# Moving one V unit into the attention loop, overlapping the closing part of a cross-covariance attention kernel, and halving its last store

## The chip, the cores and the metric

One core of one Trainium2 chip. The metric is the device time of one execution in microseconds. Each kernel is run several times; the profile ("the trace") comes from one execution and covers a span about 1.8 us shorter than the device time. For the kernel before, that execution is none of the timed runs quoted below: it took 144.34 us. Times quoted are medians of all runs. A run over 1.5% above the fastest of its kernel counts as slow and stays out of the ratios. A ratio is the mean time of one kernel's fast runs over the mean of the other's fast runs in the same rounds, so it is not quite the ratio of the medians quoted.

## The reference

```python
Q, K, V: (8, 12, 512, 64) float32
Q_norm = Q / (norm(Q, axis=-2) + 1e-10)          # norm over the 512 rows, per column
K_norm = K / (norm(K, axis=-2) + 1e-10)
attn   = einsum('bhnd,bhne->bhde', Q_norm, K_norm)          # 64 x 64 per head
attn   = softmax(attn, axis=-1)
out    = einsum('bhnd,bhde->bhne', V, attn)
```

The attention matrix is only 64 x 64 per head, but it needs all of Q and K of that head before any output of that head can be made. 96 heads are taken four at a time: 24 units.

## The kernel before

The engines: PE does the matmuls and PE transposes, ScalarE (ACT in the profile's lines), VectorE (DVE) and GpSimd (POOL) the elementwise work, SyncE (SP) issues the transfers. Matmul results land in PSUM, a small memory of which the kernel has few tiles; an eviction is the copy of outputs from PSUM to SBUF, from where they are stored.

Per unit there are two chains. The attention side: load Q and K (512 KB each), cast to bf16, gram matrices on PE, norms, scale, softmax. The V side: load V, cast (`cast_v`), eight PE transposes into PSUM and a copy out (`vtrans`), sixteen output matmuls and two evictions (`outs`), store. The program order is written by hand; the V side runs behind the attention at a rate that `outs_by` fixes.

```python
    vbp = ctx.enter_context(tc.tile_pool(name="vbp", bufs=3))
    ps_v = ctx.enter_context(tc.tile_pool(name="ps_v", bufs=1, space=bass.MemoryType.PSUM))   # one transposing tile
    ps_o = ctx.enter_context(tc.tile_pool(name="ps_o", bufs=2, space=bass.MemoryType.PSUM))
    def outs_by(s):
        return max(0, (s - 2) * 19 // 22)
    ...
    for s in range(U):                       # U = 24
        n0, n1 = outs_by(s - 1), outs_by(s)
        on(load_qk, s + LOAD_AHEAD)          # 3 ahead
        while nv < min(U, n1 + 3):
            load_v(nv); nv += 1
        while nst < n1 - 3:
            store(nst); nst += 1
        ...                                  # casts, grams, norms; outs(n0..n1-1); softmax; vtrans
    ...                                      # remaining loads and stores
    # closing part
    both = (nc.scalar.copy, nc.vector.tensor_copy)
    ...                                      # softmax of the last unit
    normalise(last - 1)
    doubled(last - 1)
    outs(n1)
    store(n1)
    normalise(last)
    doubled(last)
    for u in range(n1 + 1, U):
        cast_v(u, nc.vector.tensor_copy)
        vtrans(u)
        outs(u, both)
        store(u)
```

All loads and stores are issued by SyncE, in program order.

## Time and profile before

143.5 us (median of 4 runs, 142.95 to 145.23; the longest is a slow one, the mean of the other three is 143.3). What matters of its profile, with "E" for the start of the exponentials of unit 23, the last attention unit (all in us from the span's start):

| | before |
|---|---|
| span of the profiled run | 142.6 |
| Q of unit 23 landed / cast | 102.55 / 103.03 |
| E | 113.67 |
| last eviction ends | 138.88 (E + 25.2) |
| last store issued / landed | 138.95 / 141.72 |

The landing of a transfer is the last of its sixteen landing records in the trace, one for each DMA engine. A line of the timeline gives start, duration, engine, line of the kernel, operation, tiles as out<-in, and in brackets the idle time of the engine before it and what ended it. PEclk is the granted clock, the share of PE's full clock that the trace records, in tenths; it is 1.0 or 0.5. The page's busy shares say little here, as no engine is above 71%:

```profile
PE 89.9 (63%) x2232; PEld 70.0 (49%) x2232; DVE 101.3 (71%) x370; ACT 91.2 (64%) x159; POOL 42.3 (30%) x41
```

They average over a loop in which the transfers never pause and a closing part in which every engine mostly waits; the prediction below takes the two apart.

### The profile page before, as it was taken

Reading aid. Unit: us, or ns where it says so; the run is one execution under the profiler, and the core shown is the slowest. Engines: PE = TensorE matmul, PEld = TensorE weight load, DVE = VectorE, ACT = ScalarE, POOL = GpSimd, SP = SyncE. Lnnn points to the kernel's source line nnn. Section 1 sums busy time; section 2 is a strip of 40 time slices with the busy share of each in tenths; the row PEclk is TensorE's granted clock in tenths of the full one; section 3 lists DMA queues with packets and bytes.
Section 4 is the critical chain, followed back from the end, with each engine's and each line's share of the span. In section 5 each row is a group of like instructions: output and inputs, shape, how many; then the busy total and the mean of one; then the engine's idle time right before and its main releaser. Section 6 shows DMA issues by size and latency. Waiting matters only on the chain.

```text
span 142.6 us, 5388 instructions
## 1 busy us (share of the span) xinstructions
PE 89.9 (63%) x2232; PEld 70.0 (49%) x2232; DVE 101.3 (71%) x370; ACT 91.2 (64%) x159; POOL 42.3 (30%) x41
## 2 busy tenths in 40 slices
PE   0057746698675754889398955899559473544440
PEld 0046533586554543768285834687438342333320
DVE  0867399879999979989698999979997553123310
ACT  3013422498999965798879874998989853423340
POOL 8614233334422234442245223464321200000000
PEclk9999999999999999857975799658995955555555
DMA  4999999999999999999999999999999998533033
GB/s 176 315 406 406 398 409 410 398 399 402 401 405 403 417 401 415 395 407 413 407 416 405 407 414 408 411 407 408 405 403 404 398 402 336 221 150 142 29 123 147
DMA packets 19992, 50.67 MB, mean 355 GB/s; under 512 B 1536, under 2 KB 1536, under 8 KB 19968
## 3 DMA queue, kind: packets, MB, share of 16 engines
q1 hardware_dynamic: 19968, 50.34, 90.7%
q8 instruction: 17, 0.28, 0.8%
q14 instruction: 7, 0.06, 0.1%
HBM read 37.75 MB, written 12.58 MB: 353 GB/s over the span
## 4 chain that ended last, share of the span: by engine, by line
DVE 32%; PE 22%; POOL 17%; DMA 11%; issue 8%; ACT 4%; SPq 2%; POOLq 1%; ACTq 0%; DVEq 0%
POOL rq L111 17%; DVE scr L106 9%; DMA qf<-in_Q_dram 9%; PE po L163 7%; PE vps L145 6%; PE gram L94 6%; DVE kqs L116 5%; DVE ab L138 5%; DVE esum L134 5%; ACT vt L147 3%; DMA out_dram<-so 2%; DVE rinv L136 2%; PE lgdup L122 2%; DVE vb L87 2%; PE lgdup L152 2%
## 5 line engine op out<-in xcount | busy, mean ns | idle before, releaser
L111 POOL TENSOR_TENSOR rq<-nsq,mhalf 128x4 f32<-128x4 f32 x24 | 37.1, 1548 | 69.3 <-DVE nsq L106 69.3
L94 PE MATMUL gram<-qkb 32*128 32x128 bf16 x1536 | 36.7, 262 | 14.9 <-DVE qkb L83 9.7
L94 PEld LDWEIGHTS <-qkb 32*128 32x128 bf16 x1536 | 30.9, 117 | 16.5 <-DVE qkb L83 10.6
L147 ACT COPY vt<-vps 128x1024 bf16<-128x1024 bf16 x24 | 24.1, 1003 | 9.9 <-PE vps L145 9.6
L167 ACT COPY so<-po 128x512 f32<-128x512 f32 x43 | 23.3, 589 | 4.3 <-PE po L163 3.9
L106 DVE CUSTOM_DVE_ANT_0 scr<-gram,ident 128x128 f32<-128x128 f32 x96 | 21.9, 281 | 3.8 <-PE gram L94 3.6
L163 PEld LDWEIGHTS <-vt 128*64 128x64 bf16 x384 | 15.2, 136 | 19.1 <-ACT vt L147 11.8
L145 PE MATMUL vps<-identb,vb 128*128 128x128 bf16 x192 | 19.4, 260 | 6.6 <-DVE vb L87 5.6
L163 PE MATMUL po<-ab,vt 128*64 128x128 bf16 x384 | 19.8, 263 | 5.8 <-ACT vt L147 5.8
L80 DVE CAST qkb<-qf 128x1024 bf16<-128x1024 f32 x24 | 18.0, 749 | 7.1 <-DMA qf<-in_Q_dram 7.1
L87 ACT CAST vb<-vf 128x1024 bf16<-128x1024 f32 x19 | 19.9, 1046 | 2.9 <-DMA vf<-in_V_dram 2.9
L145 PEld LDWEIGHTS <-vb 128*128 128x128 bf16 x192 | 14.3, 116 | 10.1 <-DVE vb L87 6.8
L152 PE MATMUL lgdup<-ab,identb 64*64 64x256 bf16 x24 | 7.8, 324 | 17.3 <-DVE ab L138 17.1
L153 ACT CAST ab<-lgdup 64x256 bf16<-64x256 f32 x24 | 8.8, 368 | 14.1 <-PE lgdup L152 13.5
L83 DVE CAST qkb<-kf 128x1024 bf16<-128x1024 f32 x24 | 16.4, 683 | 0.0
L99 ACT COPY kq<-gram 64x256 f32<-64x256 f32 x24 | 8.8, 368 | 11.2 <-DVE nsq L106 10.9
L167 DVE COPY so<-po 128x512 f32<-128x512 f32 x5 | 3.5, 691 | 16.8 <-PE po L163 16.8
L122 PE MATMUL lgdup<-ident,kqs 64*64 64x64 f32 x96 | 11.4, 248 | 3.5 <-ACT ab L153 2.3
L126 DVE TENSOR_TENSOR sl<-lgdup,rq 64x256 f32<-64x256 f32 x24 | 9.9, 413 | 4.9 <-PE lgdup L122 4.7
L130 ACT ACTIVATE ex<-sl 64x256 f32<-64x256 f32 x24 | 10.0, 417 | 4.1 <-DVE sl L126 3.8
L116 DVE TENSOR_TENSOR kqs<-kq,rq 64x256 f32<-64x256 f32 x24 | 10.1, 422 | 2.3 <-POOL rq L111 0.8
L122 PEld LDWEIGHTS lgdup<-ident,kqs 64*64 64x64 f32 x96 | 7.0, 121 | 7.7 <-ACT ab L153 4.8
(16 smaller groups left out, 44.3 us busy)
## 6 DMA issues: line engine op xcount, KB each, us to landing
qf<-in_Q_dram SPq DMA_DIRECT2D x24, 512.0 KB, 10.1
kf<-in_K_dram SPq DMA_DIRECT2D x24, 512.0 KB, 10.1
vf<-in_V_dram SPq DMA_DIRECT2D x24, 512.0 KB, 10.1
out_dram<-so SPq DMA_DIRECT2D x24, 512.0 KB, 10.1
```

Source lines behind the costliest of these rows:

```text
L80: nc.vector.tensor_copy(qkb[u][:, :, 0:D], qf[u])
L83: nc.vector.tensor_copy(qkb[u][:, :, D:], kf[u])
L87: copy(w.rearrange("p s t d -> p s (t d)"), vf[u])
L94: nc.tensor.matmul(gbuf[:, h, 0:2 * D], x, x, start=(t == 0), stop=(t == R - 1), tile_position=(NV * h, 0))
L106: nc.vector.tensor_tensor_reduce(out=scr, in0=gbuf[:, h, 0:2 * D], in1=ident, scale=1.0, scalar=1e-20, op0=ALU.mult, op1=ALU.add, accum_ou ...
L111: nc.gpsimd.tensor_tensor(out=r, in0=n2, in1=mhalf, op=ALU.pow)
L116: nc.vector.tensor_tensor(out=kk[D:], in0=kq[u][D:], in1=rq[u][D:, :, None].to_broadcast([D, HU, D]), op=ALU.mult,)
L122: nc.tensor.transpose(lg[:, h, :], kqs[u][D:, h, :], ident[D:, D:])
L145: nc.tensor.transpose(ps[:, g, t, :], vb[u][:, g, t, :], identb)
L147: nc.scalar.copy(w, ps)
L163: nc.tensor.matmul(po[rows, t, :], vt[u][:, g, t, rows], a[:, 2 * g + x].rearrange("p a d -> p (a d)"), tile_position=(0, MV * x),)
L167: copies[g](s[:, g], po)
```

## The change

Its intent: do one more V unit in the loop (10/11 instead of 19/22 of the attention's rate: 19 units of outputs instead of 18), so that one unit less is left; in the closing part, put the cast and the transposes of a unit ahead of the outputs of the one before it, so that they overlap; halve the last store, so that less data follows the last eviction.

```diff
-    vbp = ctx.enter_context(tc.tile_pool(name="vbp", bufs=3))
+    vbp = ctx.enter_context(tc.tile_pool(name="vbp", bufs=4))
-        return max(0, (s - 2) * 19 // 22)
+        return max(0, (s - 2) * 10 // 11)
-    def store(u):
-        nc.sync.dma_start(out=Of[u], in_=so[u].rearrange("p s t d -> p s (t d)"))
+    def store(u, g=slice(0, SV)):
+        nc.sync.dma_start(out=Of[u][:, g], in_=so[u][:, g].rearrange("p s t d -> p s (t d)"))
     exps(last)
+    cast_v(n1 + 1, nc.vector.tensor_copy)
     normalise(last - 1)
     doubled(last - 1)
-    outs(n1)
+    vtrans(n1 + 1)
+    outs(n1, both)
     store(n1)
     normalise(last)
     doubled(last)
+    cast_v(n1 + 2, nc.vector.tensor_copy)
     for u in range(n1 + 1, U):
-        cast_v(u, nc.vector.tensor_copy)
-        vtrans(u)
+        if u + 1 < U:
+            vtrans(u + 1)
+        if u + 2 < U:
+            cast_v(u + 2, nc.vector.tensor_copy)
         outs(u, both)
-        store(u)
+        if u < last:
+            store(u)
+    for g in range(SV):
+        store(last, slice(g, g + 1))
```

## The prediction

> **What bounds the kernel now.** I read the page's forty slices first, to see where the span changes character, then the DMA issues of SyncE in order of time, then what ScalarE waits for at the end of the main loop, then one period of the closing part.
>
> ```profile
> PEclk9999999999999999857975799658995955555555
> DMA  4999999999999999999999999999999998533033
> GB/s 176 315 406 406 398 409 410 398 399 402 401 405 403 417 401 415 395 407 413 407 416 405 407 414 408 411 407 408 405 403 404 398 402 336 221 150 142 29 123 147
> ```
>
> A slice is 142.6/40 = 3.57 us. From slice 3 to slice 33, that is from 7 to 118 us, the DMA moves some 405 GB/s without a break; in the last seven slices it falls to a third. So there are two regimes: a main loop in which the transfers are always behind, and a closing part of about 25 us in which they are not. Next: who is slow in each.
>
> ```profile
> 92.51 0.34 SPq L68 DMA_DIRECT2D qf<-in_Q_dram  x1
> 93.77 0.49 SPq L69 DMA_DIRECT2D kf<-in_K_dram  x1
> 95.08 0.38 SPq L73 DMA_DIRECT2D vf<-in_V_dram  x1
> 96.37 0.39 SPq L76 DMA_DIRECT2D out_dram<-so  x1
> 97.55 0.37 SPq L73 DMA_DIRECT2D vf<-in_V_dram  x1
> ...
> 105.20 5.36 SPq L73 DMA_DIRECT2D vf<-in_V_dram  x3
> 110.61 28.71 SPq L76 DMA_DIRECT2D out_dram<-so  x9
> ```
>
> These are SyncE's issues. They come every 1.28 us, which is what 512 KB takes at 405 GB/s, and the page gives 10.1 us from issue to landing: eight transfers are always in flight and the ninth waits. So in the main loop a transfer lands according to its place in SyncE's order. The landing records of the trace say how close the compute is to them: Q of unit 10 is cast 6.3 us after it landed, Q of unit 20 0.07 us after, Q of unit 23 0.5 us after (landed 102.55, cast 103.03). An attention step takes 3.98 us (4.70 in a half-clock stretch), the four transfers of a step 5.1 us, so the loads' lead is used up just at the end.
>
> ```profile
> 105.22 1.05 ACT L87 CAST vb<-vf 128x1024 bf16<-128x1024 f32 x1 [0.52 <-DMA vf<-in_V_dram]
> 106.28 0.37 ACT L153 CAST ab<-lgdup 64x256 bf16<-64x256 f32 x1
> ```
>
> There the load is ahead on the path: the cast of V of unit 17 starts when it has landed (105.14), the copy behind it on ScalarE frees the PSUM tile for which the next logits wait (106.71), and grams, norms and exponentials of unit 23 follow without slack. The chain of waits runs through exactly these.
>
> ```profile
> 129.51 0.68 DVE L87 CAST vb<-vf 128x1024 bf16<-128x1024 f32 x1
> 130.25 1.03 PE L145 MATMUL vps<-identb,vb 128*128 128x128 bf16 x8 [1.39 <-DVE vb L87]
> 131.37 1.01 ACT L147 COPY vt<-vps 128x1024 bf16<-128x1024 bf16 x1 [2.31 <-PE vps L145]
> 132.44 1.06 PE L163 MATMUL po<-ab,vt 128*64 128x128 bf16 x16 [1.16 <-ACT vt L147]
> 133.12 0.59 ACT L167 COPY so<-po 128x512 f32<-128x512 f32 x1 [0.73 <-PE po L163]
> 133.55 0.69 DVE L167 COPY so<-po 128x512 f32<-128x512 f32 x1 [3.36 <-PE po L163]
> ```
>
> One unit of the closing part, in order of time. Nothing overlaps: cast, eight transposes, copy, outputs, eviction, and the next unit's cast comes only at 134.16, behind the eviction on VectorE. The period is 134.16 - 129.51 = 4.65 us, and there are five such units (19 to 23). Their inputs landed long before (V of unit 23 at 117.9, cast at 134.2), so this is pure latency.
>
> **What the Trainium skill says.** "TensorE: Matmul & The Clock Gate", Part 1: the PE clock is halved until about one window of 3.4 us has been busy. The trace agrees in kind: 0.5 from 114.9 us to the end, where PE works 2.1 us of 4.65. The same page, Part 4, says that transposes do not count as busy in the same way; half of the closing part's PE work is transposes, so I don't count on a warm clock there. "DMA: Bandwidth & Descriptors", Where 436 GB/s comes from: 435 GB/s is the fabric's ceiling; here 405 is the plateau, so the loop has no transfer rate to gain. The same page, Anatomy of one DMA (written for the GpSimd path): a fixed cost of about 2 us, mostly the receipt of the last write. The last store here is issued at 138.95 and has landed at 141.73, 2.8 us, of which 1.3 is the data.
>
> **The change part by part.**
>
> *Rate 10/11.* By the formula, 19 units of output instead of 18 are done in the loop, so 20 V units instead of 19 are cast and transposed there. One unit moves from the closing part. But from step 17 on one more V load and one more store stand in SyncE's order ahead of Q and K of units 21 to 23: 2 x 1.28 = 2.57 us. Setting the new order against the landing times of the same places gives Q 21, 22, 23 at 95.02, 100.07, 105.14 against casts at 94.69, 98.88, 103.03: late by 0.3, 1.2 and 2.1 us. In the middle (Q 14 to 17) the shift is the same, but there the slack left is at least 0.66 us, so it costs nothing. On ScalarE the place of V 17 in the next-to-last step is now V 18's, which lands at 107.67 instead of 105.14: 2.53 us. That is the later of the two, so the exponentials of unit 23 start not at E = 113.67 but at about 116.2. Cost: +2.5 us. The extra V work in a step costs nothing of its own there: the full-clock step was 3.98 us with V work and without.
>
> *Closing part, counted from E.* VectorE now casts V 20 (0.68) ahead of the normalisation of unit 22, whose weights are therefore ready at E + 1.7 (before: E + 0.9). PE: duplicate, transposes of V 20 from E + 2.0, outputs of 19 from 3.0 to 4.0. VectorE evicts half of it to E + 4.7 and only then normalises unit 23 (1.05 us), to E + 5.7; casts V 21 to E + 6.4. From there the pipeline runs: transposes of u+1 (1.03) and outputs of u (1.06) back to back on PE, and the copy of u+1 (1.01) and half an eviction (0.59) on ScalarE beside them. The one transposing PSUM tile is free again 1.1 us after its transposes end, just when the outputs do: period about 2.2 us. Transposes of V 21, 22, 23 begin at E + 6.5, 8.65 and 10.85; outputs of 22 end at 13.0. Outputs of 23 need the PSUM half which ScalarE frees at 13.6 (it copies V 23 first), so they run from 13.65 to 14.7, and the last eviction ends at E + 15.5. Before it ended at 138.88 - 113.67 = E + 25.2. Gain: 9.7 us.
>
> *Last store halved.* The second half carries 0.65 us of data less, but store 22 (issued at E + 13.8) and the first half are still ahead of it: I give it E + 17.7 landed against 2.85 us after the eviction before. Gain: 0.7 us. What follows the landing (0.83 us to the span's end) stays.
>
> *A fourth vb buffer* only permits the cast two units ahead. No time of its own.
>
> Sum: +2.5 - 9.7 - 0.7 = -7.9 us; 143.8 - 7.9 = 135.9. If the gate opens once PE is dense (some 5 us from E + 6.5 on), transposes and outputs shrink to 0.62 and 0.64 and the last units gain up to 1 us; I take a third of that: **135.6 us**.
>
> **Rivals.** (a) The shift doesn't reach the end, because the loads still lead: 133. For it, the list of waits has only five waits of casts on loads in the whole run (three of VectorE, two of ScalarE); against it, the slacks of 0.07 to 0.5 us. (b) The delayed loads cost more than their places: the last steps at half clock, the cast of V 18 pushing a whole ScalarE step, +4 to +5 instead of +2.5: 138. (c) The transfers take over as the end. All 96 transfers in an unbroken row: store 17, the ninetieth, lands at 121.8, six more at 1.28 us make 129.5, plus 0.83 a span of 130.3. The compute ends later than that (116.2 + 15.5 = 131.7), so the transfers are near, but not the bound; were each store to wait in a queue, 137. (d) The pipeline doesn't form, since the single transposing tile and ScalarE's order (copy before eviction) serialise it: a period of 3.2 instead of 2.2 over four units, +4: 139.5.
>
> **Range and chances.** (a) and a warm clock together give about 132.8, (b) or (d) alone 138 to 139.5. The three runs of before differ by 1.6%, which is 2.3 us. I take 132.8 to 138.8. The 2% line is 140.9; reaching it needs (b) and (d) at once: faster 0.94, same 0.05, slower 0.01.
>
> **What would show it.** Right: issues of SyncE at 1.28 us to beyond 105, Q of unit 23 landing near 105 and its cast waiting for it, V 18's cast on ScalarE waiting for its load near 107.7; exponentials of unit 23 near 116; starts of the transposes in the closing part 2.2 us apart, the last eviction some 15.5 us after those exponentials; no long gap on PE from E + 6.5 on. Wrong: exponentials of unit 23 still at 113.7 (a); periods over 3 us with PE waiting for the copy (d); a last store that lands over 3 us after its issue (c).

## The result, and the profile after

136.52 us (median of 4 runs, 135.77 to 136.9) against 143.5; ratio of the fast runs 0.952 [0.946, 0.958]. The changed kernel was run again as a control, six runs on another chip: 136.01 us, ratio 0.945 [0.942, 0.948]. So the change is worth 4.8 to 5.5%.

| us | before | predicted | after | control |
|---|---|---|---|---|
| span of the profiled run | 142.6 | 134.7 | 134.6 | 134.4 |
| Q of unit 23 landed | 102.55 | 105.14 | 104.85 | 104.26 |
| E | 113.67 | 116.2 | 115.77 | 115.61 |
| last eviction ends, after E | 25.2 | 15.5 | 15.54 | 15.52 |
| last store landed, after the last eviction | 2.84 | 2.2 | 2.33 | 2.33 |

(The predicted span is 142.6 - 7.9; 2.2 is the predicted E + 17.7 less E + 15.5.) The page of the changed kernel, the slices (3.36 us each now):

```profile
PEclk9999996558999779975797579985556985555555
DMA  4999999999999999999999999999999999975465
GB/s 150 377 396 410 401 408 414 399 401 399 402 392 413 408 407 415 400 405 412 414 403 412 413 404 405 408 412 404 410 408 410 402 407 401 405 306 205 156 247 220
```

The full-rate stretch is as long as before in microseconds (to slice 35, 118 us); what is gone is most of the slow tail: five slices after it, 17 us, where there were seven, 25 us. The granted clock at the end is 0.5 in this run.

ScalarE at the end of the loop, the line to set beside the cast of V of unit 17 in the kernel before, and then the chain of waits there:

```profile
107.43 1.05 ACT L87 CAST vb<-vf 128x1024 bf16<-128x1024 f32 x1 [1.06 <-DMA vf<-in_V_dram]
```

```profile
87.21 10.06 DMA vf<-in_V_dram
97.27 0.02 issue
97.29 0.02 SPq L73
97.30 0.03 issue
97.33 10.07 DMA vf<-in_V_dram
107.40 0.02 issue
107.43 0.59 ACT vb L87
```

In the chain (start, duration, what) two V loads of 10 us each now stand in a row on the path, and between them no cast but SyncE (SPq L73): the issue of V 18 waited until V 16, the eighth transfer before it, had landed at 97.27. The load of V 18 landed at 107.40, the cast began at 107.43. It was not only this one: from V 14 to V 18 every V cast began within 0.02 us of its load's landing. The list of waits gives 7.2 us of ScalarE waiting for V loads in the whole run, against 2.9 before. So the loop is now paced by its transfers to the last step.

The closing part, PE and ScalarE in the pipelined stretch (start, duration, engine, line, what; in brackets the idle time before it and what ended it):

```profile
122.07 1.04 PE L145 MATMUL vps<-identb,vb 128*128 128x128 bf16 x8 [0.19 <-DVE vb L87]
123.03 1.06 PE L163 MATMUL po<-ab,vt 128*64 128x128 bf16 x16
123.49 1.01 ACT L147 COPY vt<-vps 128x1024 bf16<-128x1024 bf16 x1 [1.21 <-PE vps L145]
124.40 0.59 ACT L167 COPY so<-po 128x512 f32<-128x512 f32 x1
124.55 1.01 PE L145 MATMUL vps<-identb,vb 128*128 128x128 bf16 x8 [0.45 <-ACT vt L147]
125.49 1.06 PE L163 MATMUL po<-ab,vt 128*64 128x128 bf16 x16
125.66 1.01 ACT L147 COPY vt<-vps 128x1024 bf16<-128x1024 bf16 x1 [0.67 <-PE vps L145]
126.72 1.01 PE L145 MATMUL vps<-identb,vb 128*128 128x128 bf16 x8 [0.16 <-ACT vt L147]
```

The transposes of a unit begin 2.17 us after those of the unit ahead (126.72 - 124.55; the first period is 2.48), where it was 4.65. PE runs transposes and outputs nearly back to back, and what it waits for, 0.45 and then 0.16 us, is the copy out of the one transposing tile.

Ahead of that stretch is a hole that the prediction had on its list (there PE's outputs of unit 19 end at E + 4.0 and its next transposes begin at E + 6.5; measured E + 3.9 and E + 6.3):

```profile
119.74 0.69 DVE L167 COPY so<-po 128x512 f32<-128x512 f32 x1 [2.43 <-PE po L163]
...
120.99 0.42 DVE L138 TENSOR_TENSOR ab<-ex,rinv 64x256 bf16<-64x256 f32 x1
121.33 1.28 DVE L87 CAST vb<-vf 128x1024 bf16<-128x1024 f32 x2
121.46 0.42 PE L152 MATMUL lgdup<-ab,identb 64*64 64x256 bf16 x1 [1.76 <-DVE ab L138]
```

VectorE sat idle for 2.43 us until it could evict outputs 19, and only behind that eviction normalised unit 23, whose exponentials had long been there; PE, in program order, waited 1.76 us for that. This became an experiment.

### The profile page after: what moved, and what is told of

It reads as the page before. It is cut to its first block, busy times and chain, and to the rows that moved or that the text cites. A ratio compares the mean times of both kernels' runs of the same rounds, so it can differ in the third digit from the quotient of the medians.

```text
span 134.6 us, 5372 instructions
## 1 busy us (share of the span) xinstructions
PE 92.6 (69%) x2232; PEld 72.0 (54%) x2232; DVE 101.3 (75%) x369; ACT 91.7 (68%) x160; POOL 41.0 (30%) x41
## 4 chain that ended last, share of the span: by engine, by line
DMA 32%; DVE 23%; PE 15%; POOL 11%; ACT 7%; issue 6%; SPq 3%; POOLq 0%; ACTq 0%
DMA vf<-in_V_dram 23%; POOL rq L111 11%; DMA qf<-in_Q_dram 8%; DVE scr L106 7%; PE vps L145 5%; PE po L163 4%; DVE esum L134 4%; DVE ab L138 4%; PE gram L94 4%; DVE kqs L116 3%; ACT so L167 2%; ACT vt L147 2%; DVE rinv L136 2%; DVE so L167 2%; PE lgdup L122 2%
## 5 line engine op out<-in xcount | busy, mean ns | idle before, releaser
L111 POOL TENSOR_TENSOR rq<-nsq,mhalf 128x4 f32<-128x4 f32 x24 | 35.8, 1493 | 72.3 <-DVE nsq L106 72.3
L94 PE MATMUL gram<-qkb 32*128 32x128 bf16 x1536 | 37.3, 264 | 14.6 <-DVE qkb L83 9.5
L87 ACT CAST vb<-vf 128x1024 bf16<-128x1024 f32 x20 | 20.9, 1046 | 7.2 <-DMA vf<-in_V_dram 7.2
L163 PEld LDWEIGHTS <-vt 128*64 128x64 bf16 x384 | 15.9, 139 | 11.3 <-issue 6.0
L145 PE MATMUL vps<-identb,vb 128*128 128x128 bf16 x192 | 20.0, 267 | 2.1 <-ACT vb L87 1.3
L163 PE MATMUL po<-ab,vt 128*64 128x128 bf16 x384 | 20.7, 268 | 1.0 <-DVE so L167 0.8
L152 PE MATMUL lgdup<-ab,identb 64*64 64x256 bf16 x24 | 8.1, 339 | 16.5 <-DVE ab L138 16.2
L145 PEld LDWEIGHTS <-vb 128*128 128x128 bf16 x192 | 14.9, 120 | 7.5 <-issue 4.1
L122 PE MATMUL lgdup<-ident,kqs 64*64 64x64 f32 x96 | 11.9, 256 | 3.8 <-ACT ab L153 3.4
L138 DVE TENSOR_TENSOR ab<-ex,rinv 64x256 bf16<-64x256 f32 x24 | 10.0, 417 | 0.8
```

The source lines that it names most:

```text
L87: copy(w.rearrange("p s t d -> p s (t d)"), vf[u])
L94: nc.tensor.matmul(gbuf[:, h, 0:2 * D], x, x, start=(t == 0), stop=(t == R - 1), tile_position=(NV * h, 0))
L111: nc.gpsimd.tensor_tensor(out=r, in0=n2, in1=mhalf, op=ALU.pow)
L122: nc.tensor.transpose(lg[:, h, :], kqs[u][D:, h, :], ident[D:, D:])
L138: nc.vector.tensor_tensor(out=a[0:D, :, 0, :], in0=ex[u], in1=ri[:, :, None].to_broadcast([D, HU, D]), op=ALU.mult)
L145: nc.tensor.transpose(ps[:, g, t, :], vb[u][:, g, t, :], identb)
```

## The experiments

Two questions: is the account of the parts right (the rate costs 2 us at one end and saves a unit at the other; the overlap is what gains), and is its reading of what bounds the new kernel right. Eleven kernels were run (one is the changed kernel itself, two are repetitions); all gave correct results. E1 to E4, E5 to E7 and C1 to C4 each shared a chip and the runs of the kernel before (144.0 to 144.1 us there).

**E1: the rate alone.**

```diff
 # kernel before
-        return max(0, (s - 2) * 19 // 22)
+        return max(0, (s - 2) * 10 // 11)
```

> The 10/11 rate alone, in the kernel before, with its closing part as it was. Theory: the exponentials of unit 23 start 2.1 us later than before (115.8 us against 113.7), because Q, K and V of the last units stand two transfers later in SyncE's order; the closing part loses one unit of 4.65 us; net -2.5 us, a time near 141.0 us, ratio to before about 0.982. Rival A: the later start is not due to the order of the transfers and is absent here (exponentials of unit 23 at 113.7): 138.9 us, ratio 0.968. Rival B: the rate is the main part of the change: below 138.

Measured: 141.95 us against 144.10, ratio 0.985 [0.982, 0.988]. Q of unit 23 landed at 104.77, E = 116.19, the last eviction at E + 20.6. PE in the closing part:

```profile
123.48 1.03 PE L145 MATMUL vps<-identb,vb 128*128 128x128 bf16 x8 [1.40 <-DVE vb L87]
...
128.13 1.03 PE L145 MATMUL vps<-identb,vb 128*128 128x128 bf16 x8 [1.40 <-DVE vb L87]
```

The period is still 4.65 us. The theory holds in kind: 2.5 us later at the start (2.1 were expected), one unit of 4.65 us less, 2.1 us of time gained (2.5 were expected; under the 2% line). Rival A (no later start) and B (the main part) fall.

**E2: the closing part alone, at the old rate.**

```diff
 # changed kernel
-        return max(0, (s - 2) * 10 // 11)
+        return max(0, (s - 2) * 19 // 22)
```

> The new closing part (with the halved store and four vb buffers) at the old rate 19/22. Theory: exponentials of unit 23 at 113.7 us as before; one unit more in the closing part, at 2.2 us, so the last eviction 17.7 us after those exponentials, at 131.4 us, the same as in the changed kernel; time 136.5 us, ratio about 0.952: once the closing part overlaps, the rate is worth nothing. Rival A: the rate matters also with the new closing part, and this is 2 us slower than the changed kernel: 138.5. Rival B: with the two transfers out of the way the start is earlier and the units cheap, so it is faster than the changed kernel: under 135.5.

Measured: 135.67 us, ratio 0.941 [0.938, 0.944]; E = 114.28, last eviction E + 15.90 with five units. The transposes came 2.2 us apart, as expected, but the last eviction 1.8 us earlier after E than the E + 17.7 expected: 1.2 of it because the granted clock rose to full at 126.6 us, for the last unit (see C2). The ratio was below the 0.952 of the changed kernel's first rounds, but on another chip, hence the control C1 and the repetition C2. Rival A falls; B's 135.5 was not reached.

**E3: the last store whole.**

```diff
 # changed kernel
-        if u < last:
-            store(u)
-    for g in range(SV):
-        store(last, slice(g, g + 1))
+        store(u)
```

> The changed kernel with the last store in one piece. Theory: the last eviction ends at 131.3 us as in the changed kernel, the whole store is issued after it and lands 2.8 us after its issue instead of 2.3: the span +0.5 us, time 137.0, ratio about 0.955. Rival: store 22, issued 1.3 us ahead of the first half, holds the data up anyway, and the halving is worth nothing: 136.5.

Measured: 135.96 us, ratio 0.943 [0.940, 0.947]; 137.0 was expected and 136.5 by the rival, so this came out below both. In the profile the whole store took 2.94 us from issue to landing, against 2.31 us for the second half in the changed kernel. Yet the time was no longer than that of the changed kernel. In this run the granted clock rose in the closing part and the last eviction came at E + 14.3; so one profile could not settle it. Repeated as C3.

**E4: three vb buffers.**

```diff
 # changed kernel
-    vbp = ctx.enter_context(tc.tile_pool(name="vbp", bufs=4))
+    vbp = ctx.enter_context(tc.tile_pool(name="vbp", bufs=3))
```

> The changed kernel with three vb buffers instead of four. Theory: no cast waits for a buffer, since the unit three ahead is transposed long before; same time, 136.5 us, within 0.3 us, and the cast of V 22 still right behind that of V 21. Rival: the cast two units ahead needs the fourth buffer, the casts come one unit later and the transposes of the closing part wait for them: periods over 2.5 us, +1 to +2 us.

Measured: 136.05 us (135.92 without the one slow run), ratio of the fast runs 0.942 [0.938, 0.946]; against the control's 0.945 on its chip no difference shows. The profiled run was a slow one (137.56 us), so its times are not compared; its order is: the casts of V 21 and V 22 still follow each other without a gap (122.88, 1.28 us for both) and the transposes are 2.2 us apart. The fourth buffer is not needed.

**C1: the changed kernel again (control).** No edit.

> The changed kernel again, unaltered, as the control for what follows on this chip. The earlier kernels without the rate (0.941) and without the halved store (0.943) stood nominally below the 0.952 of the changed kernel, but on another chip. If that was the chip: about 0.943 here, time near 136.0 us. If the rate or the halved store cost something: 0.952 again.

Measured: 136.01 us against 144.02, ratio 0.945 [0.942, 0.948]. The first rounds' 0.952 was chip or chance, for the most part.

**C2: the closing part alone, beside the control.** The kernel of E2.

> The new closing part at the old rate again, now beside the changed kernel on one chip. Theory (the rate is worth nothing once the closing part overlaps: 2.1 us of later start against one unit of 1.8 to 2.2 us): within 0.5 us of the changed kernel. Rival: it is 0.7 us or more faster, so the rate does harm.

Measured: 135.31 us, ratio 0.941 [0.938, 0.945]; the medians differ by 0.7 us, the means of the fast runs by 0.4% (0.941 to 0.945), and the intervals overlap. E = 114.49 against 115.61, closing part E + 16.2 against E + 15.5. But these two closing parts don't compare: in C2's profile the clock was at full from 127.0 us, in C1's it stayed at half. The transposes of unit 23, the last ones, begin within 0.4 us of where the clock rises in E2 and C2: at 126.8 and 127.3 us at the old rate (E2, C2), at 126.7 and 126.6 at the new one (changed kernel, C1). From there to the last eviction it is 3.4 us in E2 and C2 and 4.6 in the other two. So with the overlap in place no gain of the rate shows; and the nominal lead of the old rate can be the clock alone, so a cost of the rate is not shown either. The saving of a unit shrank with the unit's price, from 4.65 us to 2.2 or less, and the later start did not.

**C3: the whole store, beside the control.** The kernel of E3.

> The whole last store again beside the changed kernel on one chip. From the profiles (2.9 us from issue to landing against 2.3 us for the second half): 0.5 us slower than the changed kernel. Rival: the halving is worth nothing, within 0.2 us; what moves the time from run to run is whether the PE clock is up in the closing part.

Measured: 136.61 us, ratio 0.949 [0.946, 0.953]: nominally 0.6 us slower than the control, as expected, with intervals that just overlap; from issue to landing 2.92 us again against 2.31. But E3 had shown no loss, and the two pairs of profiles are not alike: with the whole store (E3, C3) the clock had risen before the last outputs and the stores stood closer together, in the changed kernel and C1 it had not. Like with like, counted from the last eviction to the last landing: with the clock up the whole store took 3.00 and 2.99 us (E3, C3), the halved one 2.94, 2.94 and 2.96 (E2, C2, E6). With the clock down the halved one took 2.33 twice, and no run has a whole store there. So in the profiles that compare, the halving is worth some 0.05 us; that it gains more elsewhere is not shown.

**E5: the loop's stores two units later.** A direct test of the step "the place in SyncE's order sets E":

```diff
 # changed kernel
-        while nst < n1 - 3:
+        while nst < n1 - 5:
```

> The changed kernel with the loop's stores two units later (a store is issued when five units are ahead of it instead of three). Theory: Q, K and V of the last units move two places forward in SyncE's order again, Q of unit 23 lands near 102.3 us, the exponentials of unit 23 start near 113.7 us instead of 115.8, the closing part is as long as in the changed kernel: -2.1 us, time 134.4, ratio about 0.937. The stores held back run in the closing part, where the DMA engines are half idle. Rival A: the start is set by the compute and not by the order: exponentials at 115.8, time 136.5. Rival B: the stores held back pile up ahead of the last ones, and the last store lands over 3.5 us after its issue: 136 or more, although the exponentials come earlier.

Measured: 134.42 us against 144.09, ratio 0.933 [0.928, 0.937]. Q of unit 23 landed at 102.22 instead of 104.85, E = 114.03 instead of 115.77. Nothing was computed differently; only the order of issue moved, and the start followed. Rival A falls. One profile could be chance here, for E differs by 1.7 us between profiles of one loop (E2 and C2 against C4 below, 114.3 and 114.5 against 112.8, where the edit comes after E). But over all profiles (E4's slow one left out) the two orders don't overlap: with the two transfers ahead of it (changed kernel, E1, E3, E6, C1, C3) Q of unit 23 landed at 104.3 to 105.0 us and E was 115.2 to 116.2; without (kernel before, E2, E5, E7, C2, C4) it landed at 101.8 to 102.9 and E was 112.5 to 114.5. The last store landed 2.66 us after its issue, so B falls. Q of unit 23 now waited 1.5 us for its cast: here the compute is behind again, and by this trace more room for loads would not help; no run tries it.

**E6: the normalisation of unit 23 ahead of the eviction.**

```diff
 # changed kernel
     vtrans(n1 + 1)
+    normalise(last)
+    cast_v(n1 + 2, nc.vector.tensor_copy)
     outs(n1, both)
     store(n1)
-    normalise(last)
     doubled(last)
-    cast_v(n1 + 2, nc.vector.tensor_copy)
```

> The changed kernel with the normalisation of unit 23 and the cast of V 21 put on VectorE ahead of the eviction of outputs 19. Theory: in the changed kernel PE stands from 119.7 to 121.5 us because VectorE normalises unit 23 only after that eviction; with the order turned the transposes of V 21 start near 120.0 us instead of 122.1 and all that follows is 2.0 us earlier: time 134.5, ratio about 0.938. Rival: ScalarE and the single transposing tile take over at once and less than 0.7 us is gained: 135.9 or more.

Measured: 133.84 us (133.48 without the one slow run of the four), ratio of the fast runs 0.926 [0.918, 0.933]. PE where the hole was:

```profile
118.42 1.06 PE L163 MATMUL po<-ab,vt 128*64 128x128 bf16 x16
119.42 0.42 PE L152 MATMUL lgdup<-ab,identb 64*64 64x256 bf16 x1
119.77 1.04 PE L145 MATMUL vps<-identb,vb 128*128 128x128 bf16 x8
```

From the start of outputs 19 to the next transposes it is 1.35 us, where it was 3.44 (118.63 to 122.07 in the changed kernel): 2.1 us, as expected. The wait that VectorE's order made was real and on the path. The last eviction at E + 12.25, 3.3 us sooner than in the changed kernel, has some 1.2 us of a full clock in it besides (from 123.2 us on).

**E7: E5 and E6 together.**

> Both of the last two edits together. Theory: they are independent and add up: exponentials of unit 23 near 113.7 us, last eviction 13.5 us after them; -4.1 us against the changed kernel, time 132.4, ratio about 0.923. Rival: the transfers become the end of the span (an unbroken row of all 96 would end the span near 130.3 us, 132.0 us of time), the stores wait for each other, and it is 133.5 or more.

Measured: 132.57 us (132.48 to 133.23), ratio 0.922 [0.916, 0.927], the time the theory named, but by the rival's path: the edits don't simply add up. E = 112.53, earlier than the 113.7 expected (the clock was at full from 81.0 to 111.7 us; whether that is why, no run tests), the last eviction already at 124.38, 6.9 us ahead of the changed kernel's, and the last store landed at 129.87, 5.4 us after its issue. The page:

```profile
DMA  4999999999999999999999999999999999999991
GB/s 139 391 403 406 396 410 413 402 398 398 402 397 402 404 400 408 410 396 412 403 410 411 411 413 402 413 405 413 402 417 402 409 399 406 403 405 386 371 366 59
```

No slice but the first and the last is under 0.9: this is the unbroken row of transfers of the prediction's rival (c), and the span of 130.8 us is within 0.5 us of the 130.3 worked out for it. By this trace, more speed in the closing part's compute would be worth little: its end waits for the stores ahead. No run tries it.

**C4: the order of E6 at the old rate.**

```diff
 # kernel of E6
-        return max(0, (s - 2) * 10 // 11)
+        return max(0, (s - 2) * 19 // 22)
```

> The new closing part at the old rate, with the normalisation of unit 23 and the cast of the next V ahead of the eviction. Theory: the order on VectorE gains its 2 us at either rate, and the rate still nothing: the same time as with the rate at 10/11 and the same order, 133.8 us, within 0.7. Rival: five units of outputs and loads which end near 122 us put the stores in a row behind each other and the transfers end it: 134.5 or more.

Measured: 132.66 us (132.44 to 133.27), ratio 0.922 [0.919, 0.925], 1.1 us below the 133.8 expected (within 0.7 was said, so this missed) and level with E7. It needs neither the new rate nor later stores. Against C2, which differs in the order on VectorE alone, it is 2.65 us; the profiled pair, further apart than the medians, splits into an E 1.7 us earlier (112.76), which the edit, behind E in the program, can't have made, and a closing part 2.9 us shorter (E + 13.3 with five units), less 0.7 for a last store that landed later after the last eviction (3.6 us after its issue). The clock was at full from 98.6 to 112.2 us and again from 119.1; in C2 at half from 103.1 to 127.0. How much of the 2.65 us is the clock stays open; that the order gains its 2 us is shown by the hole in E6. The full clock shows what sets the period when PE is fast:

```profile
120.92 0.61 PE L145 MATMUL vps<-identb,vb 128*128 128x128 bf16 x8 [0.50 <-ACT vt L147]
121.45 0.64 PE L163 MATMUL po<-ab,vt 128*64 128x128 bf16 x16
122.68 0.61 PE L145 MATMUL vps<-identb,vb 128*128 128x128 bf16 x8 [0.59 <-ACT vt L147]
```

The period is 1.76 us with 1.25 us of PE work in it, and PE waits 0.5 to 0.6 us for the copy of 1.01 us out of the one tile: transposes 0.61 + copy 1.01 + 0.14 between them. At the half clock the same loop gives 1.01 + 1.01 + 0.15 = 2.17, as measured in the changed kernel. So by the traces the tile and its copy bound the pipelined closing part in both states, at the half clock only just (PE alone has 2.07 us of work in 2.17). No run with a second transposing tile tests it.

E7 and C4 both beat the changed kernel by some 3.4 us. C4 is the simpler of the two: the kernel before, with the new closing part and the normalisation ahead of the eviction.

## Why the prediction was right

By its own terms, from the two profiles:

| term | predicted | measured | from |
|---|---|---|---|
| later E | +2.5 | +2.1 | 115.77 - 113.67; E5 takes most of it back by the order alone |
| closing part | -9.7 | -9.7 | 25.22 - 15.54 |
| halved store | -0.7 | -0.5 | 2.84 - 2.33 |
| landing to the span's end | 0 | +0.1 | 0.94 - 0.84 |
| sum | -7.9 | -8.0 | 142.6 - 134.6 |

- **The loop.** Places in SyncE's order carried over: V 18 was put at 107.67 and landed at 107.40, Q of unit 23 at 105.14 and 104.85. The mechanism is shown by E5, which moves nothing but issues. Not foreseen: all V casts from V 14 on, not only that of V 18, came to wait for their loads: V 14 landed as before (87.14 and 87.39) but was now cast at once, where before it had been cast a step later (91.78).
- **The middle of the run.** The shifted loads of units 14 to 17 cost nothing, as said: the least slack was 0.58 us (Q of unit 17), where 0.66 was worked out.
- **The closing part.** Right to 0.1 us, with its hole and its period. That the four-stage chain of 4.65 us, and not the number of units, was the price, is shown by E1 against E2: the rate alone gained 2.1 us, the overlap (with the halved store) 8.4 (135.67 against 144.10), of which some 1.2 can be the clock.
- **The halved store.** The 0.5 us compare a lone whole store with a halved one; that the halving made them is not shown (C3).
- **The clock.** I credited a third of a microsecond for a full clock in the closing part. The profiles of the changed kernel and of its control had none of it, although PE was busy for 6.0 of the 6.7 us from 122.07 to 128.73; the nine other profiles with the overlapped closing part all had it for some or all of their last unit. From the start of the last transposes to the last eviction it is 4.59 us at the half clock (two profiles) and 3.39 to 3.42 at the full one (seven): 1.2 us, for which up to 1 was said. What decides is not shown.
- **The number.** The credit didn't come, so 135.9 is what its terms give, and that rests on a base that doesn't fit them: the terms are from a profile of 144.34 us, the 143.8 is the median of three other runs, one of them slow. On the profile's own base the terms give 136.4, and the profiled run of the changed kernel took 136.36; so the 0.9 us between 135.6 and 136.5 are the credit and the base, not the terms. Over the fast runs the difference was 6.9 us in the first rounds (143.3 to 136.4) and 8.0 on the control's chip. That the closing part agreed to 0.1 us is partly luck: the clock had to stay at half, and of the six profiles of this closing part (changed kernel, C1, E3, C3, E4, E5) it did so in two.
- **Small slips.** The half clock begins at 114.1 us by the trace, not at 114.9, where its first slow matmuls stand. The last seven slices move 0.4 of the plateau, not a third. The lower end of the range, 132.8, comes out at 132.4 from the prediction's own terms (135.9 - 2.5 - 1.0).
- **The rivals.** (a) no later start and (d) no pipeline are excluded by the table. (b) a larger delay did not come. (c) the transfers as the end did not come in the changed kernel, but in E7, where the compute had been moved out of the way.

What the prediction did not ask: whether the first part is still worth anything once the second is there. By its own numbers, +2.5 against a unit of 2.2, the answer was in it: no, and no gain shows in C1 against C2.

## What to carry to other kernels

When the transfers of a loop are always behind, every issue put ahead of a load delays it by one transfer's time, here 1.28 us: work moved into such a loop is not free even where the engines have room, so set its place in the issue order against what the work costs outside. A closing part that runs cast, transpose, copy and output one after the other is priced by its latency; overlapping it cheapens each unit, and with it the worth of moving units elsewhere. In a part written in program order look at what stands behind an eviction on each engine: a short operation that was ready held PE up here for 1.8 us.

## What the Trainium skill lacked or had wrong

- "TensorE: Matmul & The Clock Gate", Part 4 says that the full clock does not engage for transposes, which do not count as PE-busy the same way. Here eight transposes took 1.01 to 1.04 us at the half clock and 0.61 us at the full one, and the clock went up (and, in C4, stayed up for 10 us) in a closing part of which half of the PE work is transposes. Whether the transposes or the outputs between them raised it, no run separates. It doesn't always rise: the closing part was E + 15.5 us in both profiles of the changed kernel and E + 14.3 and 14.4 in E3 and C3, which differ only in the last store, behind all of this.
- "DMA: Bandwidth & Descriptors" has two points. Its figure of about 2.0 us plus bytes over 436 GB/s (Anatomy of one DMA) is for the GpSimd path. For a store issued by SyncE, with no other transfer under way, 512 KB took 2.77 us from issue to the last landing, where the formula would give 3.2. And its best guess for DMA engines that lag (Latency and other measured facts) is tied to the GpSimd path; here all loads and stores are issued by SyncE, and still the sixteen parts of one 512 KB load landed 2.3 us apart near 50 us (Q of unit 12 in the kernel before) and 4.0 us apart late (V 18 in the changed kernel: 103.40 to 107.40), against 0.2 us for the lone last store of the kernel before. The landing records don't say which engine each part came from, and no run here shows the cause.
